# Log-sum-exp over heads: declaring the two PSUM banks of a pair independent when they hold different units of work

## The chip, the cores and the metric

The kernel runs on one core of a Trainium2 chip. The metric is the time of one execution on the device, in microseconds (us), as a median over runs. Only runs of the "fast" state are compared (for a program on one core: within 1.5% of the fastest run of the same kernel). The span of a profile is some 2 us shorter than the timed execution.

## The reference

```python
x:    (8, 2048, 2048) float32     # B, S, D
bias: (8, 256) float32            # H heads of 256
x_heads = x.reshape(B, S, H, Dh).transpose(0, 2, 1, 3) + bias[None, :, None, :]
x_tiled = np.repeat(x_heads, 2, axis=2)
mx  = x_tiled.max(axis=-1, keepdims=True)
lse = mx.squeeze(-1) + np.log(np.exp(x_tiled - mx).sum(axis=-1))   # (8, 8, 4096)
```

So 134 MB are read, each row of 256 is added to a bias, exponentiated and summed, and 1 MB of logarithms is written, each value twice.

## The kernel before

The input comes in 64 units `t`, each a tile of 128 partitions by 2 rows by 2048 columns (2 MB), in 9 buffers. Within a tile the heads are shared out over the engines: PE adds the bias to some heads in PSUM (a matmul puts the bias into a bank, a second one with the identity adds x), POOL adds it to others, and the rest is multiplied by exp(bias) afterwards on DVE. ACT takes all exponentials, DVE most sums. The shares change with the stage:

```python
BULK   = dict(pe=3, acc=1, g0=4, late=True,  fold=0)   # pe: heads that PE biases
MIXED  = dict(pe=1, acc=1, g0=4, late=False, fold=0)
PROMPT = dict(pe=2, acc=2, g0=8, late=False, fold=0)
STAGES = [(0, (BULK,)), (50, (MIXED,)), (56, (MIXED, MIXED)),
          (61, (PROMPT, PROMPT)), ...]                 # two entries: each row is a unit of its own
```

In BULK one unit fills a whole pair of banks. From unit 50 on a unit takes one bank, so that a pair holds two different units:

```python
pairs = [pp.tile([P, 2 * MM], F32, name=f"pair{i}") for i in range(2)]   # two tiles of two banks
ps = [p[:, c : c + MM] for p in pairs for c in (0, MM)]                  # four banks, in turn
...
def put_bias(m, k0, k1):          # ahead of time, for the next unit
    ...
        p = ps[n_ps[0] % len(ps)][:, 0 : (kb - ka) * n]
        nc.tensor.matmul(p, lhsT=ones3, rhs=each_row(b3, 0, n, kb - ka), start=True, stop=False)

def add_x(m, t, k0, got):         # when the unit's data is there
    ...
        mm = nc.tensor.matmul(p, lhsT=ident, rhs=xts[t % NBUF][:, ka:kb, 0:n], start=False, stop=True)
        on_x(t, mm, [loads[t, k0, 0]])

def sum_biased(m, t, k, p, mm, sums):      # ACT reads the bank
    ...
        act = nc.scalar.activation(out=xts[t % NBUF][:, k, c : c + Dh], in_=p[:, c : c + Dh],
                                   func=ACT.Exp, accum_out=sums[:, k, h : h + 1])
        last_uses[t].append(on_x(t, act, [mm]))
```

The program's waits are derived from the tiles that the instructions touch. A pair is one tile, so a read of one of its banks counts as a conflict with a write of the other. `on_x(t, ins, after)` declares an instruction on tile `t` independent of every other engine's instructions on that tile, except those in `after`. In program order the parts of a MIXED unit n are: x into bank n, bias into bank n+1, (on ACT) POOL's heads of unit n-1, the DVE-weighted heads of n, the read of bank n.

The softmax here doesn't subtract the row's maximum and nothing guards it: scores larger than these inputs give would overflow.

## Time and profile before

| | before |
|---|---|
| time, median | 327.52 us (327.4 to 327.56, 3 runs) |
| span of the profile | 325.5 us |
| granted PE clock, mean | 0.859 |
| instructions in the profile | 2113 |
| busiest engines | POOL 289.9 us, DVE 285.9 us |

The lines on which the argument rests are shown in the prediction.

### The profile page before, as it was taken

To read this page: it belongs to the slowest core of one execution; us is meant where nothing else is said; L and a number is where in the kernel's file an instruction comes from. 1 tells how busy PE (TensorE), PEld (TensorE's weight loads), DVE (VectorE), ACT (ScalarE), POOL (GpSimd) and SP (SyncE) were. 2 spreads that over 40 slices of the span, in tenths; PEclk is the share of its full clock that TensorE was granted. 3 is DMA by queue.
4 is the path that set the end of the run, shared out by engine and by line. 5 is a ranking of instruction groups with operands and counts; after the bars stand their busy time and mean duration, and the time that the engine had idled before them with its cause. 6 is when DMAs were issued, how large, how long until landed. Compare 5 with 4: busy or idle time off the path is not lost.

```text
span 325.5 us, 2113 instructions
## 1 busy us (share of the span) xinstructions
PE 250.0 (77%) x541; PEld 86.9 (27%) x541; DVE 285.9 (88%) x320; ACT 264.3 (81%) x421; POOL 289.9 (89%) x88
## 2 busy tenths in 40 slices
PE   4478999499987888777879797889788455576792
PEld 1123333233322323223323232223223101122220
DVE  1006999999999999999898899989998999999995
ACT  1119999499978969888787978697879897799995
POOL 6999999799999999999999999999999999999713
PEclk9999999899979979998997989797979855555558
DMA  8999999999999999999999999999999999999994
GB/s 293 427 431 429 431 429 424 431 427 429 429 429 429 427 426 429 429 423 430 432 425 429 431 422 427 431 427 429 429 431 425 429 432 424 413 422 421 422 400 143
DMA packets 11806, 135.42 MB, mean 416 GB/s; under 512 B 1361, under 2 KB 1489, under 8 KB 2833
## 3 DMA queue, kind: packets, MB, share of 16 engines
q1 hardware_dynamic: 11696, 135.27, 98.6%
q8 instruction: 4, 0.07, 0.1%
q14 instruction: 8, 0.07, 0.0%
q10 hardware_dynamic: 2, 0.01, 0.0%
q0 software_dynamic: 96, 0.00, 0.0%
HBM read 134.23 MB, written 1.05 MB: 416 GB/s over the span
## 4 chain that ended last, share of the span: by engine, by line
DMA 48%; DVE 33%; ACT 8%; POOL 6%; PE 3%; issue 1%; SPq 0%; DVEq 0%
DMA xt<-in_x_dram 45%; DVE R L326 27%; ACT xt L307 6%; DVE xt L319 4%; POOL xt L301 4%; DMA b<-bparts 2%; PE pair L249 1%; PE one_ps L249 1%; DVE xt L342 1%; ACT xt L282 1%; DMA brow<-in_bias_dram 1%; ACT xt L267 1%; POOL brest L173 1%; POOL brest L171 1%; PE pair L203 0%
## 5 line engine op out<-in xcount | busy, mean ns | idle before, releaser
L301 POOL TENSOR_TENSOR xt<-xt,b_rep 128x2048 f32<-128x2048 f32 (+1 forms) x66 | 277.3, 4210 | 18.9 <-DMA xt<-in_x_dram 18.9
L326 DVE TENSOR_REDUCE R<-xt 128x14 f32<-128x3584 f32 (+1 forms) x56 | 208.1, 3716 | 2.6 <-ACT xt L307 0.9
L307 ACT ACTIVATE xt<-xt 128x2560 f32<-128x2560 f32 (+3 forms) x91 | 164.2, 1828 | 14.8 <-POOL xt L301 14.3
L249 PE MATMUL pair<-xt,ident 128*128 128x512 f32 x200 | 105.5, 654 | 0.0
L249 PE MATMUL one_ps<-xt,ident 128*128 128x512 f32 x100 | 61.0, 695 | 19.9 <-DMA xt<-in_x_dram 19.8
L267 ACT ACTIVATE xt<-pair 128x1024 f32<-128x1024 f32 x50 | 52.3, 1045 | 17.2 <-PE pair L249 15.8
L249 PEld LDWEIGHTS pair<-xt,ident 128*128 128x128 f32 x200 | 42.4, 212 | 56.0 <-issue 56.0
L319 DVE TENSOR_TENSOR xt<-xt,w_ps 128x512 f32<-128x512 f32 x50 | 34.0, 680 | 25.6 <-ACT xt L307 25.4
L233 PE MATMUL pair<-xt,ident 128*128 128x512 f32 (+1 forms) x44 | 34.0, 872 | 21.2 <-DMA xt<-in_x_dram 18.2
L260 ACT ACTIVATE xt<-one_ps 128x256 f32<-128x256 f32 x100 | 37.7, 394 | 8.1 <-PE one_ps L249 8.1
L203 PE MATMUL one_ps<-b,ones 3*128 3x512 bf16 x50 | 19.0, 381 | 17.9 <-ACT xt L260 11.8
L203 PEld LDWEIGHTS <-ones 3*128 3x128 bf16 x150 | 12.5, 92 | 65.7 <-issue 59.7
L203 PE MATMUL pair<-b,ones 3*128 3x512 bf16 x100 | 29.9, 378 | 0.0
L249 PEld LDWEIGHTS one_ps<-xt,ident 128*128 128x128 f32 x100 | 15.6, 197 | 41.3 <-DMA xt<-in_x_dram 34.1
L260 ACT ACTIVATION_READ_ACCUMULATOR xt<-one_ps 128x1 f32 x100 | 22.1, 221 | 0.0
L342 DVE CUSTOM_DVE_ANT_0 xt<-xt,one_ps 128x256 f32<-128x256 f32 x50 | 19.1, 414 | 0.3 <-ACT xt L307 0.3
L233 PEld LDWEIGHTS pair<-xt,ident 128*128 128x128 f32 x44 | 10.4, 294 | 29.6 <-DMA xt<-in_x_dram 19.7
L342 DVE CUSTOM_DVE_ANT_0 xt<-xt,w_ps 128x256 f32<-128x256 f32 x45 | 17.5, 417 | 0.0
L282 ACT ACTIVATE xt<-pair 128x256 f32<-128x256 f32 x34 | 12.5, 374 | 0.1
L326 DVE TENSOR_REDUCE R_last<-xt 128x4 f32<-128x1024 f32 x10 | 12.1, 1214 | 0.0
L218 PE MATMUL pair<-b,ones 3*128 3x512 bf16 (+1 forms) x22 | 10.2, 465 | 1.1 <-ACT xt L267 1.1
L358 POOL TENSOR_TENSOR xt<-xt,w_sb 128x256 f32<-128x256 f32 (+1 forms) x2 | 2.1, 1026 | 8.7 <-ACT xt L307 8.5
(38 smaller groups left out, 55.9 us busy)
## 6 DMA issues: line engine op xcount, KB each, us to landing
xt<-in_x_dram SPq DMA_DIRECT2D x56, 2048.0 KB, 29.9
xt<-in_x_dram SPq DMA_DIRECT2D x14, 1024.0 KB, 21.0
xt<-in_x_dram SPq DMA_DIRECT2D x5, 256.0 KB, 11.4
out_dram<-res SPq DMA_DIRECT2D x1, 896.0 KB, 7.3
xt<-in_x_dram SPq DMA_DIRECT2D x2, 384.0 KB, 16.5
out_dram<-res_last SPq DMA_DIRECT2D x1, 128.0 KB, 1.7
b<-bparts POOLq DMA_DIRECT2D x3, 1.5 KB, 6.5
brow<-in_bias_dram ACTq DMA_DIRECT2D x1, 8.0 KB
```

What stands on the lines that cost most here:

```text
L203: nc.tensor.matmul(p, lhsT=ones3, rhs=each_row(b3, h * Dh, Dh, K), start=True, stop=False,)
L218: nc.tensor.matmul(p, lhsT=ones3, rhs=each_row(b3, 0, n, kb - ka), start=True, stop=False,)
L233: mm = nc.tensor.matmul(p, lhsT=ident, rhs=xts[t % NBUF][:, ka:kb, 0:n], start=False, stop=True,)
L249: mm = nc.tensor.matmul(p, lhsT=ident, rhs=xts[t % NBUF][:, :, h * Dh : (h + 1) * Dh], start=False, stop=True,)
L260: act = nc.scalar.activation(out=xts[t % NBUF][:, k, 0:Dh], in_=got[0][:, k * Dh : (k + 1) * Dh], func=ACT.Exp, accum_out=sums[:, k, 0:1],)
L267: act = nc.scalar.activation(out=xts[t % NBUF][:, :, Dh : m["pe"] * Dh].rearrange("p k (h j) -> p h k j", j=Dh), in_=got[-1].rearrange("p ...
L282: act = nc.scalar.activation(out=xts[t % NBUF][:, k, c : c + Dh], in_=p[:, c : c + Dh], func=ACT.Exp, accum_out=sums[:, k, h : h + 1],)
L301: add = nc.gpsimd.tensor_tensor(out=v, in0=v, in1=each_row(b_rep, c - G0, D - c, k1 - k0), op=ALU.add)
L307: return on_x(t, nc.scalar.activation(out=v, in_=v, func=ACT.Exp), [after])
L319: mul = nc.vector.tensor_tensor(out=f, in0=f, in1=each_row(w_ps, m["pe"] * Dh - W0, n, k1 - k0), op=ALU.mult,)
L326: red = nc.vector.tensor_reduce(out=sums[:, k0:k1, h0:H], in_=v.rearrange("p k (h j) -> p k h j", j=Dh), op=ALU.add, axis=mybir.AxisListTy ...
L342: ttr = nc.vector.tensor_tensor_reduce(out=v, in0=v, in1=w, scale=1.0, scalar=0.0, op0=ALU.mult, op1=ALU.add, accum_out=dst,)
```

## The change

Its intent: PE and ACT are not to wait for each other where they work on different banks of a pair that belong to different units. A list of the users of each pair is kept, and each new user is declared independent of the other bank's users on other engines.

```diff
+    bank_users = [[], []]
+
+    def on_bank(i, ins):
+        for j, u in bank_users[i // 2]:
+            if j != i and u.ins.engine != ins.ins.engine:
+                tc.declare_no_dep(ins.ins, u.ins, reason="another bank")
+        bank_users[i // 2].append((i, ins))
+        return ins
 ...
+                on_bank(bank, mm)                                           # put_bias
 ...
-            on_x(t, mm, [loads[t, k0, 0]])
+            on_bank(bank, on_x(t, mm, [loads[t, k0, c0]]))                  # add_x
 ...
-            last_uses[t].append(on_x(t, act, [mm]))
+        last_uses[t].append(on_bank(bank, on_x(t, act, [mm])))              # sum_biased
```

The rest of the diff (cut here) lets a unit take several banks, splits the lists of heads by column, and defers parts in the same order. None of it changes the instructions of the modes in use.

More of the change, by code (lines that the diff above doesn't have):

```diff
@@ L211, in put_bias, with add_x @@
         n = m["pe"] * Dh
-        step = MM // n
+        rows = min(k1 - k0, max(MM // n, 1))
         got = []
-        for ka in range(k0, k1, step):
-            kb = min(ka + step, k1)
-            p = ps[n_ps[0] % len(ps)][:, 0 : (kb - ka) * n]
-            n_ps[0] += 1
-            nc.tensor.matmul(
-                p,
-                lhsT=ones3,
-                rhs=each_row(b3, 0, n, kb - ka),
-                start=True,
-                stop=False,
-            )
-            got.append((ka, kb, p))
-        return got
-    def add_x(m, t, k0, got):
-        n = m["pe"] * Dh
-        rows = []
-        for ka, kb, p in got:
+        for k in range(k0, k1, rows):
+            for c in range(0, n, MM):
+                w = min(n - c, MM)
+                bank = n_ps[0] % len(ps)
+                p = ps[bank][:, 0 : rows * w]
+                n_ps[0] += 1
+                mm = nc.tensor.matmul(
+                    p,
+                    lhsT=ones3,
+                    rhs=each_row(b3, c, w, rows),
+                    start=True,
+                    stop=False,
+                )
+                on_bank(bank, mm)
+                got.append((k, k + rows, c, w, bank, p))
+        return got
+    def add_x(m, t, k0, c0, c1, got):
+        heads = []
+        for ka, kb, c, w, bank, p in got:
+            if not c0 <= c < c1:
+                continue
             mm = nc.tensor.matmul(
@@ L235, in add_x @@
                 lhsT=ident,
-                rhs=xts[t % NBUF][:, ka:kb, 0:n],
+                rhs=xts[t % NBUF][:, ka:kb, c : c + w],
                 start=False,
@@ L239, in add_x @@
             )
-            on_x(t, mm, [loads[t, k0, 0]])
-            rows += [(p[:, k * n : (k + 1) * n], mm) for k in range(kb - ka)]
-        return rows
+            on_bank(bank, on_x(t, mm, [loads[t, k0, c0]]))
+            for i in range(0, (kb - ka) * w, Dh):
+                k, cw = divmod(i, w)
+                heads.append((ka + k, (c + cw) // Dh, bank, p[:, i : i + Dh], mm))
+        return heads
     def late_heads(m, t, got, sums):
@@ L276, in late_heads, with sum_biased @@
         return pe_part
-    def sum_biased(m, t, k, p, mm, sums):
-        for h in range(m["pe"]):
-            c = h * Dh
-            act = nc.scalar.activation(
-                out=xts[t % NBUF][:, k, c : c + Dh],
-                in_=p[:, c : c + Dh],
-                func=ACT.Exp,
-                accum_out=sums[:, k, h : h + 1],
-            )
-            last_uses[t].append(on_x(t, act, [mm]))
+    def sum_biased(t, k, h, bank, p, mm, sums):
+        act = nc.scalar.activation(
+            out=xts[t % NBUF][:, k, h * Dh : (h + 1) * Dh],
+            in_=p,
+            func=ACT.Exp,
+            accum_out=sums[:, k, h : h + 1],
+        )
+        last_uses[t].append(on_bank(bank, on_x(t, act, [mm])))
     def each_row(src, c, n, k_rows):
@@ L452, with pe_part @@
             add = None
+            heads = []
             if c0 == 0:
-                if m["late"]:
-                    pe_part = late_heads(m, t, bias_there, sums)
-                else:
-                    got = add_x(m, t, k0, bias_there)
+                bias_here = bias_there
+            if m["late"]:
+                pe_part = late_heads(m, t, bias_here, sums)
+            else:
+                heads = add_x(m, t, k0, c0, c1, bias_here)
+                def pe_part(t=t, heads=heads, sums=sums):
+                    for k, h, bank, p, mm in heads:
+                        sum_biased(t, k, h, bank, p, mm, sums)
+            if c0 == 0:
                 if next_units and not m["late"]:
@@ L461 @@
                     add = g_add(m, t, k0, k1)
-            if c0 == 0 and (t < T - 1 or k0 == 0):
-                flush(for_pool)
+                if t < T - 1 or k0 == 0:
+                    flush(for_pool)
             if t == T_PROMPT and c0 == 0:
@@ L493, in pool_part @@
                     load(t + NBUF)
-            if not m["late"]:
-                def pe_part(t=t, m=m, got=got, k0=k0, k1=k1, sums=sums):
-                    for k in range(k0, k1):
-                        sum_biased(m, t, k, *got[k - k0], sums)
             for_pool.append(pool_part)
-            if c0 == 0:
-                if m["g0"] < H:
-                    pe_part()
-                    if m["late"]:
-                        bias_there = put_bias(*next_units.pop(0))
-                else:
-                    for_pe.append(pe_part)
+            if m["g0"] < H:
+                pe_part()
+                if m["late"]:
+                    bias_there = put_bias(*next_units.pop(0))
+            elif heads:
+                for_pe.append(pe_part)
         fb, at = divmod(t - 2, NBLK)
```

## The prediction

> **What bounds the kernel now.** I read the page of the kernel before first: busy time by engine, then the slices.
>
> ```profile
> PE 250.0 (77%) x541; PEld 86.9 (27%) x541; DVE 285.9 (88%) x320; ACT 264.3 (81%) x421; POOL 289.9 (89%) x88
> ...
> DMA  8999999999999999999999999999999999999994
> GB/s 293 427 431 429 431 429 424 431 427 429 429 429 429 427 426 429 429 423 430 432 425 429 431 422 427 431 427 429 429 431 425 429 432 424 413 422 421 422 400 143
> ```
>
> No compute engine is full over the span, but the DMA row is 9 from the second slice to the last but one; the stretch from 24 to 250 us, asked for by itself, moves 428 GB/s. The input alone is 134.2 MB; at 428 GB/s that is 134.2/0.428 = 313.6 us of the 325.5 us span. The remaining 12 us are the ramp at the start and the tail after the last input. So the kernel is a stream of loads with compute riding on it, and a compute change pays only if it starts a load earlier or shortens the tail.
>
> Second, where the changed code runs. The one-unit-per-pair code is used in all but the BULK stage, so from unit 50 of 64 on. The groups of instructions show it:
>
> ```profile
> L233 PE MATMUL pair<-xt,ident 128*128 128x512 f32 (+1 forms) x44 | 34.0, 872 | 21.2 <-DMA xt<-in_x_dram 18.2
> ...
> L282 ACT ACTIVATE xt<-pair 128x256 f32<-128x256 f32 x34 | 12.5, 374 | 0.1
> ...
> L218 PE MATMUL pair<-b,ones 3*128 3x512 bf16 (+1 forms) x22 | 10.2, 465 | 1.1 <-ACT xt L267 1.1
> ```
>
> L218 puts the bias into a bank, L233 adds x to it (two instructions for each unit), L282 is the exponential that reads it. All three lie after 250 us. The last columns matter most: ACT sat idle for 0.1 us in all before its 34 reads of a bank. PE sat idle for 21.2 us before its additions, but 18.2 us of it waited for the input itself.
>
> Third, who waits for whom, from 250 us to the end. For ACT alone, and for PE alone:
>
> ```profile
> ACT xt L307 <- POOL xt L301: 5.0, 10, 1.1
> ACT res_last L414 <- PE tpair L408: 0.8, 1, 0.8
> ACT res L397 <- PE tpair L387: 0.8, 1, 0.8
> ACT xt L307 <- DMA xt<-in_x_dram: 0.3, 1, 0.3
> ...
> PE pair L233 <- DMA xt<-in_x_dram: 18.2, 15, 2.4
> ...
> PE pair L233 <- ACT xt L282: 3.0, 1, 3.0
> ```
>
> ACT is the only consumer of what PE writes to these banks, and it is not listed as waiting for L233 or L218 at all: it waits for POOL, for data, and for two transposes that the change does not touch. PE waited for a bank's reader once, for 3.0 us. That is the only sizeable wait in the trace that the change can take away.
>
> Fourth, the chain that ended last, in order of time from 280 us: POOL L301, then ACT L307 and L282 back to back to 294.4 us, one load of 19.82 us to 314.24 us, ACT L307 and L282 to 318.67 us, DVE L342 to the end. No PE instruction on these banks is in that part of it.
>
> **What the Trainium skill says.** "PSUM — Partial Sum Buffer", section "PSUM bank collisions raise a hardware error": two engines on one bank and the same 32 partitions collide, while on different banks they run clean, so software is to guard by bank. Hence the guard between the two banks of a pair is not needed, and no slowdown is to be expected where PE writes one bank and ACT reads the other. The trace before agrees: counted off from unit 56, the addition at 304.33 us (1.22 us long) writes the neighbour of the bank that ACT reads at 304.35 us, and that read takes 0.36 us, like those with no write beside them. "Perfetto Trace Analysis", section "Identifying Dependency Chains": an instruction with waits on several engines may have extra event instructions put before it. The trace agrees: the line of the x additions has three such event instructions, at 259.5 us to 279.5 us, 51 ns each. "DMA: Bandwidth & Descriptors", section "Specifications": a fabric ceiling of 435 GB/s. The measured 428 GB/s agree, so there is next to nothing to win in the stream. "TensorE: Matmul & The Clock Gate", section "HAM oscillation — how this bites in real kernels": PE gaps above some 3.4 us lower its clock. The trace shows a granted clock of 0.5 from about 260 us, with idle gaps of 2.2 to 2.4 us in each 4.9 us; the gaps here are set by the input, which the change doesn't move.
>
> **The change part by part.** The rewritten bookkeeping (column loop, list of heads, order of the deferred parts) gives the same instructions in the same order for the modes in use: no mode here has over 512 columns, so each unit still takes one bank, one bias matmul, one addition, and the same reads. I count 0 instructions added. What changes is the waits. From the program order I find three kinds of wait between the two banks of a pair.
>
> (a) The addition of an odd-numbered bank waits for ACT's reads of its neighbour: units 51, 53 and 55, which are the three event instructions. From unit 56 on, neighbours are two rows of one tile, and there the helper for x has already declared them independent. Here is the one that shows as a wait, in the timeline, for PE, POOL and ACT:
>
> ```profile
> 259.85 2.07 PE L233 MATMUL pair<-xt,ident 128*128 128x512 f32 x2 [2.96 <-ACT xt L282]
> ...
> 259.50 4.55 POOL L301 TENSOR_TENSOR xt<-xt,b_rep 128x2048 f32<-128x2048 f32 x1 [0.36 <-DMA xt<-in_x_dram]
> ...
> 259.69 3.28 ACT L307 ACTIVATE xt<-xt 128x2048 f32<-128x2048 f32 x2
> 262.87 0.37 ACT L282 ACTIVATE xt<-pair 128x256 f32<-128x256 f32 x1
> ```
>
> POOL starts on the same tile at 259.50 us, so its data was there then. Of PE's 2.96 us, 2.6 us (256.9 to 259.5) would have gone to the data anyhow; the bank cost 259.85 - 259.50 = 0.35 us. The addition ended at 261.92 us. Its reader on ACT came at 262.87 us, after 3.28 us of other ACT work: 0.95 us of slack already. Starting PE 0.35 us earlier makes the slack 1.3 us. Gain on the path: 0. For unit 53 the data came at 269.73 us (POOL's start) and PE started at 269.80; ACT's reads of the neighbour had ended at 268.29. For unit 55 it is 279.52 and 279.59, the reads over at 278.31. So these lose only some 0.07 us each, which I take for the event instruction. Sum over PE: 0.35 + 2 x 0.07 = 0.5 us of idle time, none on the path.
>
> (b) ACT's read of an even bank waits for the neighbour's bias matmul, issued in between. For unit 52 that matmul ran from 266.82 to 267.42 us and the read started at 267.46. Usually such a read starts 0.1 us before the exponential before it ends (here 267.37), so at most 267.46 - 267.27 = 0.19 us were lost. But ACT then sat idle for 1.11 us until POOL let it go on at 269.41, so the gain on the path is again 0. For unit 54 the bias matmul was over at 277.21 us, the read started at 277.50; later ones have more slack.
>
> (c) The bias matmul of an even bank waits for an older read of the neighbour (three units back) rather than of its own bank (four back). The only idle before L218 is 1.1 us on L267, the bulk stage's own bank: a true dependency, which stays. Gain 0.
>
> At the very end, the last addition of x ends by 319.01 us (317.89 + 1.12) and the last four reads start at 320.10 us, behind ACT's own exponentials. PE has 1.1 us to spare there too. The sum on the path: 0 us, perhaps 0.1 us either way from jitter. Predicted time: 327.4 us.
>
> **Rivals.** First, the waits are worth more than they look: PE's earlier start carries forward, its half clock recovers, and the tail shortens. For it: PE is busy without a break from 309.4 to 316 us at clock 0.5. Against it: ACT never waits for PE there, each unit waits anew for its own data, and DVE is full from 300 to 317 us whatever PE does. I give the rival at most the 0.5 us of (a), all of it passed on to the end, so 327.0 us. Second, something gets worse: PE writes one bank while ACT reads its neighbour, and both slow down, or the changed semaphore counts add waits elsewhere. All the reads of L282 with their accumulator reads take 34 x (0.374 + 0.201) = 19.6 us; 10% on them would be 2.0 us, not all on the path, so some 328.5 us. Against it: the overlap at 304.3 us above, which cost nothing, and that on ACT waits only go away. Third, the stream is disturbed: loads are issued earlier or later and collide. But loads wait for DVE and ACT to release a tile, which (b) may move by 0.2 us at unit 52 at most, while a load takes about 20 to 30 us from issue to landing: it is queued, so nothing comes of it: 327.4 us.
>
> **Range and chances.** The three runs before spread over 0.16 us. The main case and the third rival (together 0.9) give 327.2 to 327.7; the first pulls to 327.0, the second to 328.5. I take 326.8 to 328.0 to leave room for another chip or day. To be faster by 2% the change would have to save 6.5 us, over twelve times the PE idle that I can assign to it: 0.01. Slower by 2% needs a broken overlap of 6.5 us, a third on top of all the bank reads: 0.01.
>
> **What would show it.** Right: no event instructions on the x additions; unit 51's addition starts with POOL on the same tile; PE's wait of L233 on L282 gone and turned into a wait for the input of about 2.6 us; unit 52's read up to 0.2 us earlier, followed by a longer wait for POOL; ACT's waits for POOL otherwise the same; the end at 325.5 us of span, give or take 0.3. Wrong: a new wait of ACT on PE, reads of L282 clearly over 0.37 us, or loads that land at another rhythm than one unit in 4.9 us. The prediction would be wrong if ACT's waits for POOL hid waits for PE that the profile put down to the later releaser, or if the order of instructions on an engine were not the same as before.

## More of the kernel before

One more view is of use: the busy time of the engines by stretch. The columns are the stretch, its length, then PE, PE's weight load, DVE, ACT and POOL busy (with instructions), the granted PE clock, the DMA share and GB/s.

```profile
250.00:284.00 34.00, 19.85 (x32) 5.28 (x30) 33.28 (x73) 28.93 (x44) 31.42 (x7) 0.62 1.00 425
284.00:296.00 12.00, 8.28 (x17) 3.17 (x17) 11.43 (x39) 11.90 (x22) 12.00 (x7) 0.50 1.01 420
296.00:310.00 14.00, 9.57 (x16) 3.50 (x17) 14.00 (x44) 13.14 (x23) 11.28 (x5) 0.50 1.01 422
```

The changed code runs in these stretches and in the tail behind them. The reader is to see that PE is the least busy of the four engines in each of them, at a granted clock of 0.62, 0.50 and 0.50, while the stream of loads stays full.

## The result, and the profile after

| | before | after |
|---|---|---|
| time, median of 4 runs | 327.46 us (327.27 to 327.56) | 327.38 us (327.33 to 327.72) |
| ratio | 1 | 1.0 (95% interval 0.9983 to 1.0018) |
| span of the profile | 325.5 us | 325.6 us |
| instructions in the profile | 2113 | 2110 |

A ratio is worked out by program over the fast runs of the same rounds, so it is not quite the ratio of the medians quoted. The time is the same. The lines after that answer to those in the prediction follow; line numbers have moved (L233 is now L249, L282 is L298, L218 is L231, L301 is L317, L307 is L323). First the page's busy times, DMA rate and two groups of instructions of the changed kernel.

```profile
PE 250.1 (77%) x541; PEld 87.4 (27%) x541; DVE 285.8 (88%) x320; ACT 263.7 (81%) x421; POOL 289.9 (89%) x88
...
GB/s 293 433 429 427 433 429 420 435 431 423 433 431 423 429 430 423 427 431 428 426 431 429 425 428 431 425 427 437 423 427 431 427 424 428 417 422 421 423 400 136
...
L249 PE MATMUL pair<-xt,ident 128*128 128x512 f32 (+1 forms) x44 | 33.0, 850 | 21.2 <-DMA xt<-in_x_dram 21.2
...
L298 ACT ACTIVATE xt<-pair 128x256 f32<-128x256 f32 x34 | 12.5, 374 | 0.0
```

No counted instruction was added or taken away on a compute engine: x541, x320, x421 and x88 as before; the three instructions fewer in all are the event instructions on the additions. The additions of x still have 21.2 us of idle time before them, to the tenth the number of before (that is chance: with only PE's half of the change, below, it is 21.7 us), but now all of it is a wait for the input. The reads on ACT take 374 ns, as before, though they now may run beside a write of the neighbouring bank. Next, who waited for whom from 250 us to the end, for PE and for ACT of the changed kernel (total us, times, longest).

```profile
PE pair L249 <- DMA xt<-in_x_dram: 21.2, 17, 2.6
...
PE pair L231 <- ACT xt L285: 1.5, 1, 1.5
...
ACT xt L323 <- POOL xt L317: 4.4, 9, 1.0
ACT xt L285 <- PE pair L267: 1.8, 1, 1.8
```

PE's wait of 3.0 us for a bank's reader is gone: before, 18.2 us for the input and 3.0 us for ACT; after, 21.2 us for the input. The removed wait has turned into a wait for the data that would have come next anyhow. ACT's waits for POOL are 5.0 us before and 4.4 us after. ACT's wait of 1.8 us for PE belongs to the BULK stage (L285), in which the change has no part, and comes before the first unit of the new kind. Last, the timeline of unit 51 of the changed kernel: PE, POOL, ACT.

```profile
259.53 2.07 PE L249 MATMUL pair<-xt,ident 128*128 128x512 f32 x2 [2.40 <-DMA xt<-in_x_dram]
...
259.55 4.54 POOL L317 TENSOR_TENSOR xt<-xt,b_rep 128x2048 f32<-128x2048 f32 x1 [0.35 <-DMA xt<-in_x_dram]
...
259.73 0.36 ACT L298 ACTIVATE xt<-pair 128x256 f32<-128x256 f32 x1
...
263.62 0.37 ACT L298 ACTIVATE xt<-pair 128x256 f32<-128x256 f32 x1
```

PE starts with POOL on the new tile (259.53 and 259.55 us) instead of 0.35 us after it. The read at 259.73 us is of unit 50's bank, the neighbour of the bank that PE is writing at that moment; it takes 0.36 us. Unit 51's own read comes at 263.62 us, 2.0 us after the addition's end (259.53 + 2.07 = 261.60).

### The profile page after: what moved, and what is told of

Its sections match the earlier page's. It is cut to its first block, busy times and chain, and to the rows that moved or that the text cites. A ratio compares the mean times of both kernels' runs of the same rounds, so it can differ in the third digit from the quotient of the medians.

```text
span 325.6 us, 2110 instructions
## 1 busy us (share of the span) xinstructions
PE 250.1 (77%) x541; PEld 87.4 (27%) x541; DVE 285.8 (88%) x320; ACT 263.7 (81%) x421; POOL 289.9 (89%) x88
## 4 chain that ended last, share of the span: by engine, by line
DMA 48%; DVE 33%; ACT 8%; POOL 6%; PE 3%; issue 1%; SPq 0%; DVEq 0%
DMA xt<-in_x_dram 45%; DVE R L342 27%; ACT xt L323 6%; DVE xt L335 4%; POOL xt L317 4%; DMA b<-bparts 2%; PE pair L267 2%; PE one_ps L267 1%; DVE xt L358 1%; ACT xt L298 1%; DMA brow<-in_bias_dram 1%; ACT xt L285 1%; POOL brest L171 1%; POOL brest L173 1%; PE pair L214 0%
## 5 line engine op out<-in xcount | busy, mean ns | idle before, releaser
L317 POOL TENSOR_TENSOR xt<-xt,b_rep 128x2048 f32<-128x2048 f32 (+1 forms) x66 | 277.4, 4212 | 18.8 <-DMA xt<-in_x_dram 18.8
L323 ACT ACTIVATE xt<-xt 128x2560 f32<-128x2560 f32 (+3 forms) x91 | 164.3, 1829 | 13.5 <-POOL xt L317 13.1
L285 ACT ACTIVATE xt<-pair 128x1024 f32<-128x1024 f32 x50 | 52.5, 1050 | 17.2 <-PE pair L267 16.1
L249 PE MATMUL pair<-xt,ident 128*128 128x512 f32 (+1 forms) x44 | 33.0, 850 | 21.2 <-DMA xt<-in_x_dram 21.2
L249 PEld LDWEIGHTS pair<-xt,ident 128*128 128x128 f32 x44 | 10.2, 288 | 29.4 <-DMA xt<-in_x_dram 29.2
L298 ACT ACTIVATE xt<-pair 128x256 f32<-128x256 f32 x34 | 12.5, 374 | 0.0
L413 ACT ACTIVATE res<-tpair 64x512 f32<-64x512 f32 x7 | 4.1, 590 | 8.9 <-PE tpair L403 8.7
L231 PE MATMUL pair<-b,ones 3*128 3x512 bf16 (+1 forms) x22 | 10.0, 455 | 1.5 <-ACT xt L285 1.5
```

Of the source, the lines that this page charges most:

```text
L231: mm = nc.tensor.matmul(p, lhsT=ones3, rhs=each_row(b3, c, w, rows), start=True, stop=False,)
L285: act = nc.scalar.activation(out=xts[t % NBUF][:, :, Dh : m["pe"] * Dh].rearrange("p k (h j) -> p h k j", j=Dh), in_=got[-1].rearrange("p ...
L298: act = nc.scalar.activation(out=xts[t % NBUF][:, k, h * Dh : (h + 1) * Dh], in_=p, func=ACT.Exp, accum_out=sums[:, k, h : h + 1],)
L317: add = nc.gpsimd.tensor_tensor(out=v, in0=v, in1=each_row(b_rep, c - G0, D - c, k1 - k0), op=ALU.add)
L323: return on_x(t, nc.scalar.activation(out=v, in_=v, func=ACT.Exp), [after])
```

## The experiments

My theory was that the freed waits end before ACT's own queue reaches the bank, so that nothing can come of them. The rivals were that only the stream of input hides a gain, and that a gain is there but is given back by something else. Each experiment ran beside runs of the kernel before on the same chip; where a ratio is given, it is to those.

### Only PE's half, only ACT's half

```diff
-            if j != i and u.ins.engine != ins.ins.engine:
+            if j != i and u.ins.engine != ins.ins.engine and <ins is PE's>:          # a_only
+            if j != i and u.ins.engine != ins.ins.engine and <ins is ACT's>:         # b_only
```

> The changed kernel with only PE's instructions declared independent of the other bank's readers; ACT's reads keep their waits for the neighbour's matmuls. My theory (the freed waits end before ACT's own queue gets to the bank): no event instructions on the x additions, unit 51's addition starts within 0.05 us of POOL's start on the same tile, 327.4 us give or take 0.4. The rival (the gain comes and is given back by the reads on ACT): a time over 0.5 us under the kernel before's, since the part that could give it back is missing.

> The changed kernel with only ACT's reads declared independent of the neighbour's matmuls; PE's instructions keep their waits. My theory: the three event instructions and the 0.35 us wait at unit 51 are back, 327.4 us give or take 0.4. The rival: over 0.5 us slower than the kernel before.

Measured, one execution each: 327.34 us and 327.40 us, with the kernel before at 327.6 us (327.45 to 327.71, 7 runs). In the first, unit 51's addition starts at 259.58 us and POOL at 259.60 us, and there are no event instructions. In the second the three event instructions are back, and so is the wait, with 3.47 us longer than in the kernel before. The timeline of the second, PE, POOL and ACT:

```profile
261.11 2.07 PE L249 MATMUL pair<-xt,ident 128*128 128x512 f32 x2 [3.47 <-ACT xt L298]
...
259.32 4.54 POOL L317 TENSOR_TENSOR xt<-xt,b_rep 128x2048 f32<-128x2048 f32 x1 [0.38 <-DMA xt<-in_x_dram]
...
264.12 0.37 ACT L298 ACTIVATE xt<-pair 128x256 f32<-128x256 f32 x1
```

The bank held PE up by 261.11 - 259.32 = 1.79 us here, five times the 0.35 us of the kernel before. The addition still ended at 263.18 us, 0.94 us before its reader came, and the time is the same. The slack stays the same because the late read and the next one move together: ACT always has 3.28 us of other work between them, and the addition takes 2.07 us. So neither half shows a gain that the other gives back, as far as one execution each can tell: the rival wanted over 0.5 us, and the kernel before spreads over 0.26 us in the same rounds.

### The stream taken away

```diff
         for k0, k1, c0, c1 in pieces(t):
+            if t >= NBUF and k1 - k0 == K:
+                k1 = k0 + 1                      # load one row of two; wrong on purpose
 ...                                              # and scale=0.01 in the exponentials
```

> The kernel before with every load from unit 9 to unit 55 cut to one row of the two (1 MB in place of 2 MB), results wrong on purpose, exponents scaled by 0.01 so that the rows not loaded stay finite. The stream of loads is then no longer the limit. Both theories: 300 to 312 us, with POOL (4.54 us a unit) or DVE as the limit, and PE's additions wait for the bank's reader and not for data. It is the base for the same cut of the changed kernel.

> The changed kernel with the same cut of the loads. My theory (PE's additions are early because ACT comes to the bank over 3 us after the neighbour's reads, by its own order): within 0.3% of the cut kernel before, though PE's waits for readers shrink. The rival (only the stream of input hides the gain): 1 to 6 us faster than the cut kernel before, as the three additions no longer wait.

> The cut kernel before, run again behind its partner: 315.3 to 318 us.

> The changed kernel with the loads cut, run again ahead of its partner, because the first time it came out 0.5% slower than the cut kernel before, with profiles of the same span. My theory (ACT and DVE have the same rhythm in both, so the difference is scatter of a kernel that is no longer paced by its loads): within 0.3% of the partner. The rival (letting PE run up to three units ahead costs something): again 0.4% or more slower.

Measured: 316.34 us (315.33 to 316.62) for the cut kernel before and 317.29 us (316.49 to 318.35) for the cut changed kernel; run again, 317.49 us and 317.71 us. Ratios to the kernel before of the same rounds are 0.965 and 0.9696 the first time, 0.9688 and 0.9702 the second. The results were wrong, as intended, and by the same error in both. The first pair missed my 0.3% (0.9696/0.965 is 0.5% slower, and the 95% intervals, 0.9634 to 0.9667 and 0.9672 to 0.9719, do not meet), the second is within it (0.9702/0.9688 is 0.14% slower, the intervals overlap), and the cut kernel before differs from itself by about as much between the two series (0.965 and 0.9688). I read that as scatter; a loss of 0.1 to 0.5% through the change is not excluded here, a gain is not seen. The time missed my 300 to 312 us: POOL is full until 275.7 us, and then come the last units, which were laid out for a slower stream and take DVE and ACT 30 of 30 us each from 270 to 300 us.

The trace is what decides. The timeline of the cut kernel before, PE and then ACT:

```profile
250.94 2.07 PE L235 MATMUL pair<-xt,ident 128*128 128x512 f32 x2 [2.85 <-ACT xt L286]
...
258.75 2.08 PE L235 MATMUL pair<-xt,ident 128*128 128x512 f32 x2 [3.01 <-ACT xt L286]
...
253.95 0.39 ACT L286 ACTIVATE xt<-pair 128x256 f32<-128x256 f32 x1
...
257.83 0.40 ACT L286 ACTIVATE xt<-pair 128x256 f32<-128x256 f32 x1
```

And the same of the cut changed kernel:

```profile
247.84 2.08 PE L251 MATMUL pair<-xt,ident 128*128 128x512 f32 x2
250.38 2.08 PE L251 MATMUL pair<-xt,ident 128*128 128x512 f32 x2
...
253.76 0.39 ACT L302 ACTIVATE xt<-pair 128x256 f32<-128x256 f32 x1
...
257.65 0.40 ACT L302 ACTIVATE xt<-pair 128x256 f32<-128x256 f32 x1
```

With the data there in advance, PE of the kernel before waits some 3 us for a bank's reader at each odd unit. The changed kernel's PE doesn't, and runs ahead: unit 51 at 247.84 us instead of 250.94, unit 52 at 250.38 instead of 253.48. It then waits at later bias matmuls for a bank to come free: from 220 us to the end 10.1 us in all, against 4.9 us in the kernel before. ACT comes to the banks of units 51 and 52 in the same rhythm in both: 257.83 - 253.95 = 3.88 us and 257.65 - 253.76 = 3.89 us. So even the 3 us, with no input to hide them, are worth nothing. The rival that only the stream hides the gain wanted the changed kernel 1 to 6 us faster here. It falls. What the cut does not show is a stage in which nothing but PE is short of time: ACT has no idle time from 248.7 to 300 us in either trace, so a full ACT stands here in the place of the stream.

### The stage made longer

```diff
-    (50, (MIXED,)),
+    (4, (MIXED,)),
```

> The kernel before with the stage of one head a unit on PE (MIXED) begun at unit 4 in place of unit 50, so that 26 units and not 3 have the event instruction and the wait of an odd bank for its neighbour's reads. Both theories: POOL at 4.54 us, DVE at some 4.4 us and ACT at 4.0 us a unit still fit under the 4.9 us that a unit takes to load, so 325 to 330 us.

> The changed kernel with the same long stage, so that the gain or loss for each unit is multiplied by more than eight. My theory: within 0.2% (0.65 us) of the long kernel before. The rival that the 0.35 us of PE's wait and 0.07 us of an event instruction do reach the end: 26 x 0.07 to 26 x 0.35 us, that is 1.8 to 9 us faster.

Measured: 331.52 us (331.2 to 331.79) and 331.6 us (331.06 to 331.67), ratios 1.012 and 1.0118. I had given 325 to 330 us for the first, which was 1.5 us too low. The kernel before has 26 event instructions on its additions here, the changed kernel none, and the times agree to 0.1 us. The rival wanted 1.8 to 9 us. From 40 to 280 us, PE's waits before its additions are 87.9 us for the input and 16.6 us for ACT in the first (104.5 us), and 101.6 us for the input alone in the second.

This run also shows the other direction, ACT waiting for the neighbour's bias matmul. The timeline of ACT in the long kernel before:

```profile
150.86 0.38 ACT L282 ACTIVATE xt<-pair 128x256 f32<-128x256 f32 x1 [0.61 <-PE pair L218]
...
152.80 3.28 ACT L307 ACTIVATE xt<-xt 128x2048 f32<-128x2048 f32 x2 [1.10 <-POOL xt L301]
```

And in the long changed kernel:

```profile
150.19 0.38 ACT L298 ACTIVATE xt<-pair 128x256 f32<-128x256 f32 x1
...
152.66 3.28 ACT L323 ACTIVATE xt<-xt 128x2048 f32<-128x2048 f32 x2 [1.63 <-POOL xt L317]
```

Such waits are few: 1.3 us at two reads from 40 to 280 us. The 0.61 us wait is gone, and the wait for POOL right behind it has grown from 1.10 to 1.63 us. POOL waits for the data. What the bank gives, the next wait takes.

### How much later may PE be?

```diff
+            for z in range(NZERO if m["pe"] == 1 else 0):    # 2 or 4; units 50 to 60
+                mm = nc.tensor.matmul(p, lhsT=ones3, rhs=zer[:, ...], start=False, stop=z == NZERO - 1)
```

Matmuls of zeros behind the addition of x make the bank ready later, with the right sums.

> The kernel before with two matmuls of zeros put behind the addition of x to each bank in units 50 to 60 (each some 0.6 us at the half clock for 512 columns, 0.4 us for 256), so that the bank is ready 0.8 to 1.2 us later; the sums stay right. My theory: the slack (0.95 us at unit 51, and ACT's wait of about 1 us for POOL behind each read) takes it up: 327.5 us give or take 0.7, with ACT now listed as waiting for PE at some reads. The rival (PE sets the pace in this stage and the waits between banks cost time through it): 2 us or more above the kernel before.

> The changed kernel with the same two matmuls of zeros. My theory: 327.5 us give or take 0.7 and within 0.3% of the same edit of the kernel before. The rival: 0.5 to 3 us faster than the same edit of the kernel before.

> The kernel before with four matmuls of zeros: from the data's landing the bank takes some 2.07 + 4 x 0.60 = 4.5 us at the half clock, against 2.7 us until ACT comes to it now, so the slack is used up, ACT waits for PE, and units 53 and 55 start behind ACT's late reads of the neighbour. Both theories: slower than the kernel before, by 0.5 to 7 us, unless the clock rises as PE fills up.

> The changed kernel with four matmuls of zeros. Here the waits between banks can lie on the path, if they ever do: my theory has it 0 to 1 us faster than the same edit of the kernel before (two units at up to 0.5 us each); the rival 1 to 4 us faster.

| | before with the zeros | changed with the zeros |
|---|---|---|
| two | 327.33 us (327.16 to 327.43), ratio 0.9992 | 327.52 us (327.37 to 327.61), ratio 0.9996 |
| four | 328.93 us (328.41 to 330.46), ratio 1.0049 | 327.69 us (327.28 to 327.88), ratio 1.0002 |

Two zeros a unit cost nothing in either kernel. ACT is now listed as waiting for PE at reads of these banks, 0.9 us in all in the kernel before, and its waits for POOL shrink to 3.0 us: the slack is used. With four, the changed kernel still holds, and the kernel before loses. Here, and only here, the change is worth something: the medians differ by 1.2 us, the ratios by 0.47% (about 1.5 us), and the 95% intervals of the ratios do not meet (1.002 to 1.0077 and 0.9987 to 1.0016). That is a little more than the 0 to 1 us I had allowed and within the rival's 1 to 4 us, so for a PE this full the rival's mechanism is right. The timeline with four zeros, first the kernel before (PE in units 52 and 53, POOL at unit 53, ACT's read of unit 52):

```profile
265.97 2.08 PE L236 MATMUL pair<-xt,ident 128*128 128x512 f32 x2
267.98 1.88 PE L245 MATMUL pair<-zer,ones 3*128 3x512 bf16 x4
269.66 0.63 PE L221 MATMUL pair<-b,ones 3*128 3x512 bf16 x1
271.22 2.08 PE L236 MATMUL pair<-xt,ident 128*128 128x512 f32 x2 [0.93 <-ACT xt L293]
...
269.43 4.54 POOL L312 TENSOR_TENSOR xt<-xt,b_rep 128x2048 f32<-128x2048 f32 x1 [0.36 <-DMA xt<-in_x_dram]
...
270.32 0.38 ACT L293 ACTIVATE xt<-pair 128x256 f32<-128x256 f32 x1 [0.66 <-PE pair L221]
```

Then the changed kernel, unit 53:

```profile
269.49 2.07 PE L252 MATMUL pair<-xt,ident 128*128 128x512 f32 x2 [0.57 <-DMA xt<-in_x_dram]
```

In the kernel before a loop has closed: PE adds x, puts the neighbour's bias, ACT waits for that bias, reads, and only then may PE start the neighbour's addition. The two engines take turns, and PE lags the data. POOL began unit 53's tile at 269.43 us, so PE is 1.79 us late; in the changed kernel it starts with the data. (Four zeros took 1.88 us, not the 4 x 0.60 us of my expectation.) What I had left out of my expectation is unit 51: it already starts 261.73 - 259.44 = 2.29 us after POOL, behind ACT's late read of unit 50, and PE does not catch up afterwards, being busy 25.87 of the 26 us from 284 to 310 us. In that kernel the chain that ended last runs through PE's additions to 318.25 us; in the changed one they end at 316.78 us, 1.47 us earlier. The edit has a flaw that I had not foreseen: the zeros are not passed through `on_x`, so in the kernel before they wait for the neighbour's reads also in units 56 to 60, where the additions themselves do not. It hardly counts: PE came to unit 56 at 284.75 us, against 283.32 us in the changed kernel, so 1.43 us of the 1.47 us were lost before; the one such wait that shows, at 288.42 us, is some 0.13 us.

## Why the prediction was right

- **The bound.** The stream carries 413 to 437 GB/s in every slice but the first and the last two, in both. The predicted 327.4 us met 327.38 us; that it is so close is luck, as the four runs of each kernel spread over 0.3 to 0.4 us.
- **(a), the additions on PE.** Right in mechanism, and in size for the trace that it was read from; the 0.35 us is no constant, as the run with only ACT's half has 1.79 us in its place. PE's start moved onto POOL's (259.53 and 259.55 us), and 2.40 us of the wait stayed as a wait for the data, where I had said about 2.6 us. Units 53 and 55 start 0.02 and 0.03 us before POOL (269.59 and 269.61; 279.37 and 279.40), against 0.07 us after it, so an event instruction cost nearer 0.1 us than the 0.07 us I gave. That the slack on ACT, not the data, makes all this worthless was a step of the working; the runs with the loads cut show it.
- **(b), the reads on ACT.** Right that it is absorbed by the wait for POOL. The size at unit 52 could not be read from the changed kernel, since ACT came to it later in that run (its exponentials ended at 267.61 us, the bias matmul at 267.30 us). The long stage shows it: 0.61 us gained, 0.53 us more wait for POOL.
- **(c), the bias matmuls.** Right in the time, incomplete in the count. I expected waits to go and none to come. In the compiled programs 8 of the 22 bias matmuls carry a wait for ACT before, and 19 after: the wait for the reader of the bank's own last use was implied before by the neighbour's wait, and must now be stated. In the changed kernel none of the added waits shows as idle time; L231 waits once, 1.5 us for the BULK stage's bank (L285), a true dependency that was there before (1.1 us).
- **The tail.** Right. The last chain is the same piece by piece: a load that lands at 314.16 us (314.24 before), ACT to 318.60 us (318.67), then DVE.
- **A slip of words.** Where the prediction says "one-unit-per-pair code", it should say one unit per bank; it is BULK that gives a unit a whole pair.
- **The rivals.** Slower reads beside a write: not seen, 374 ns on average in both. A disturbed stream: not seen, the rate is as above. An earlier PE that carries forward: its condition is that PE sets the pace, which needed four more matmuls a unit.

## What to carry to other kernels

Before removing a wait, look at what its waiter would wait for next, and at when the waiter's own consumer gets there; if the idle time in front of the group would only change its releaser, as here from 18.2 + 3.0 us to 21.2 us, the time will not change. A conflict between two halves of one tile costs something once producer and consumer take turns through it and the producer has no idle time left; adding cheap work to the producer until the time moves tells how far away that is. Here the margin was at least two small matmuls a unit in either kernel and at least four with the change (where PE is already on the chain that ended last), so the change buys room for more work on PE, not time.

## What the Trainium skill lacked or had wrong

- "Perfetto Trace Analysis", section "Identifying Dependency Chains" tells of the extra event instructions but not of their cost: the record is 51 ns long, and the matmul behind it starts about 0.1 us later than without it. The section "Matmuls" of the same page advises rotating through different banks. It does not say that two banks in one allocated tile can still be tied together by waits: with PE full that cost 1.2 us here (medians 328.93 and 327.69 us).
- "TensorE: Matmul & The Clock Gate", section "What's actually happening" has the full clock come back after some 3.4 us of sustained activity. In the changed kernel with four matmuls of zeros, PE is recorded busy 26.00 of 26 us from 284 to 310 us, and the granted clock stays at 0.50 all that time. A busy row of PE alone does not tell the clock; why it stayed low is open. The section "HAM oscillation — how this bites in real kernels" of the same page, which the prediction cites, ties the lowered clock to PE gaps above some 3.4 us. The trace before does not agree: the clock is 0.50 from 258 us on, some 1 us into a gap of 2.96 us (256.9 to 259.85 us), and stays there to 306 us with gaps of at most 2.4 us.
